# A hybrid decoder layer on one core: the attention's matmul order fixed to the source's, last products moved back, PSUM reads regrouped, and q's and k's parts written straight to their places

## The chip, the core and the metric

The kernel runs on one core of one Trainium2 chip. The metric is the device time of one execution in microseconds (us); lower is better. A core has TensorE (PE: matrix products and transposes), VectorE (DVE), ScalarE (ACT), GpSimd (POOL) and SyncE (SP: transfers). Each has its own instruction queue, and waits on the others through semaphores.

## What is computed

One layer on a sequence of 1024 positions, width 1024, everything in float32:

```python
hn = rms_norm(h, norm1_g[i])
proj = hn @ w_in[i]            # split into a_b, a_c, a_h, q, k, v, c_u, c_v
y_a = a_b * short_conv(a_c * a_h, conv_w[i])
q = rms_norm(q, per head);  k = rms_norm(k, per head)
y_b = stick_breaking_attention(q, k, v)          # 8 heads x 64
y_c = spatial_gating(gelu(c_u), gelu(c_v), ...)
h = h + concat(y_a, y_b, y_c) @ w_out[i]
h = h + square(relu(rms_norm(h, norm2_g[i]) @ w_ff1[i])) @ w_ff2[i]
h = h + sigmoid(rms_norm(h, norm3_g[i]) @ w_ple_gate[i]) * (p[i] @ w_ple_proj[i])
```

Only the attention concerns us. For a query t and the keys s < t, with z = q.k / 8, it is

```python
log_rem = where(causal, log_sigmoid(-z), 0)
suffix = cumsum of log_rem from the right, without the own term
weights = where(causal, exp(log_sigmoid(z) + suffix), 0);  o = weights @ v
```

so a weight is sigmoid(z) times the product of sigmoid(-z) over the later keys: two sigmoids, a running product from the right, and one multiplication.

## The kernel before, in words

**Number format.** A float32 operand is cut into a high and a low part (`split`, L135: ScalarE writes the high part, VectorE the difference), and a product is the three matmuls high by high, high by low and low by high (`product`, L161).

**Stages.** First come the gate's projection (`pp_ps`) and the spatial gate's (`vu_ps`, `gating`); then the stage in question, in which the attention's four pairs of heads are projected and worked on, followed by the convolution's projections; then the output projection (`o_ps`), the squared-ReLU layer (`f_ps`, `d_ps`) and the gate (`g_ps`).

**Projection, `project(pr)`, L343.** For each pair of heads the weights are loaded and split (`load_w`: `whi`, `wlo`), and for each block t of 128 positions 24 matmuls sum q, k and v of the pair into a bank `qkv_ps` (two banks, pool `ps_mm`). After that, in the source's order: ScalarE writes the squares (`qk_sq`, L373 and L374), VectorE sums them (`ss`, L377), GpSimd raises to -0.5 (`rs`, L174), VectorE scales q and k (`qk`, L382), and last v is cut into its parts (`V`, L141 by ScalarE and L142 by VectorE). `qk` and `V` read the same bank, and the tool that sets the semaphores keeps accesses of two engines to one bank in the source's order.

**Turning, `turn_qk`, L394.** After every second block q and k are transposed (`qk_tr`, L401, one of the three banks of pool `ps_tr`) and stored as operands. For head 0 an operand `QS[0]` holds q's high part in its 64 partitions and q's low part in the other 64; `KH[0]` holds k's high part twice; `KL[0]` holds k's low part and zeros; head 1 has the same with the halves exchanged. Before, whole 128-partition parts are written first (`QS[0]`, `q_lo`, `KH[0]`, and the two halves of `KL`), and after every fourth block six copies move them to their places (ScalarE L411 to L413, VectorE L414 to L416).

**Attention, `attend(pr)`, L421.** A step is a head and a group g of two query blocks t = 2g, 2g+1; the groups go 0, 1, 2, 3 for the first head and 3, 2, 1, 0 for the second. `stick` makes the weights of a step: for each t, and for each half of the keys, matmuls into a bank `z` (two banks, pool `ps_z`), two sigmoids by ScalarE (`rem`, `wt`; L454, L455), the running product by VectorE (L459), and the multiplication by VectorE or GpSimd (L462). `gather` multiplies them with v: `turn(j)` transposes four blocks of weights into a bank of `ps_tr` (`w_tr`, L484), which are split (`wT_hi`, `wT_lo`), and four to two matmuls per key block sum into `av` (L502), two turns behind; then `av` is read out. `attention` (L525) runs the stick of step i+1, then the gather of step i.

**Weaving.** Both are generators that yield after each piece with its cost in units. `weave` (L267) alternates between the attention of a pair and a filling stream: the projection of the next pair, and for the fourth pair the convolution. The projection of the first pair runs before (`alone`). `later` puts the turning 72 units behind its block; what is still waiting when a pair of heads ends is issued at once (L701). The order in which the source issues is not the order in which an engine works: a scheduler picks among what is ready by its own estimate of time, and each engine then works through its list without changing it.

## Time and profile before

| | us |
|---|---|
| median of 3 runs | 1221.15 (1217.46 to 1222.93) |
| the profiled execution | 1216.81 |
| its span, from the first to the last instruction | 1214.9 |
| busy in the span: PE / PE's weight loads (PEld) | 1191.8 / 1018.2 |
| busy in the span: DVE / ACT / POOL | 886.8 / 629.1 / 400.9 |

The attention stage lies at about 105 to 410 us. A row of the view of stretches gives the stretch, its length, then for PE, PEld, DVE, ACT and POOL the busy time in it and in brackets how many instructions started, then the clock that TensorE was granted as a share of the full one, the share of the DMA engines and GB/s. A row of the view of groups gives line, engine, operation, output and inputs with shapes, the count, the busy time and the mean duration of one in ns, and behind the second bar how long the engine stood idle before them and for what.

### The profile page before, as it was taken

How to read it: one execution, taken by the hardware profiler on the slowest of the kernel's cores; microseconds unless marked ns; L12 is line 12 of the kernel's file. 1: busy time of each engine (PE TensorE's matmuls, PEld its weight loads, DVE VectorE, ACT ScalarE, POOL GpSimd, SP SyncE). 2: the span in 40 equal slices, each digit the busy share in tenths (PEclk: the TensorE clock that was granted, in tenths of full speed). 3: DMA queues.
4: the chain of work that ended last, by engine and by line, in shares of the span. 5: the costliest groups of instructions: out<-in, count | busy, mean ns of one | idle time of the engine just before them, and what ended most of it. 6: DMA issues, size and time to landing. Idle time of an engine off the chain costs nothing.

```text
span 1214.9 us, 17743 instructions
## 1 busy us (share of the span) xinstructions
PE 1191.8 (98%) x5852; PEld 1018.2 (84%) x5852; DVE 886.8 (73%) x1310; ACT 629.1 (52%) x1244; POOL 400.9 (33%) x408
## 2 busy tenths in 40 slices
PE   9999899999999999999999999999999999999997
PEld 7899899898988888888888888888888888888886
DVE  7846888988887657877878768787665556753597
ACT  7736767667764355744333333356443444546542
POOL 3324345365343312124453544421023301013412
PEclk9999999999999999999999999999999999999998
DMA  9602359999554786779999899778889985654857
GB/s 318 222 18 94 124 166 267 247 184 171 132 116 101 164 287 207 198 194 269 251 256 251 231 261 258 217 249 277 321 248 313 279 264 171 217 163 112 179 160 208
DMA packets 127964, 254.04 MB, mean 209 GB/s; under 512 B 14496, under 2 KB 22432, under 8 KB 127168
## 3 DMA queue, kind: packets, MB, share of 16 engines
q1 hardware_dynamic: 94992, 168.08, 41.8%
q0 software_dynamic: 27664, 57.05, 25.0%
q10 hardware_dynamic: 5216, 27.79, 6.4%
q8 instruction: 46, 0.75, 0.2%
q14 instruction: 46, 0.38, 0.1%
HBM read 192.30 MB, written 92.80 MB: 235 GB/s over the span
## 4 chain that ended last, share of the span: by engine, by line
PE 86%; DVE 5%; DMA 4%; POOL 1%; issue 1%; ACT 1%; SPq 0%; ACTq 0%; DVEq 0%; POOLq 0%
PE f_ps L812 25%; PE d_ps L812 25%; PE g_ps L812 6%; PE qkv_ps L165 3%; PE qkv_ps L166 3%; PE qkv_ps L167 3%; PE av L502 2%; PE w_tr L484 2%; DVE rem L459 1%; PE vu_ps L167 1%; PE vu_ps L166 1%; PE vu_ps L165 1%; PE o_ps L167 1%; PE o_ps L165 1%; PE o_ps L166 1%
## 5 line engine op out<-in xcount | busy, mean ns | idle before, releaser
L139 DVE TENSOR_TENSOR w_lo<-raw,w_hi 128x512 fp32r<-128x512 f32 x280 | 245.1, 879 | 88.1 <-ACT w_hi L138 86.4
L138 ACT CAST w_hi<-raw 128x512 fp32r<-128x512 f32 x280 | 171.9, 619 | 232.6 <-PE d_ps L812 112.6
L812 PE MATMUL f_ps<-hn_hi,w_hi 128*128 128x512 f32 x448 | 175.1, 392 | 0.0
L812 PE MATMUL d_ps<-f_hi,w_hi 128*128 128x512 f32 x448 | 174.8, 390 | 0.0
L812 PE MATMUL f_ps<-hn_lo,w_hi 128*128 128x512 f32 x448 | 174.7, 390 | 0.0
L812 PE MATMUL f_ps<-hn_hi,w_lo 128*128 128x512 f32 x448 | 174.5, 390 | 0.0
L812 PE MATMUL d_ps<-f_hi,w_lo 128*128 128x512 f32 x448 | 174.3, 389 | 0.0
L812 PE MATMUL d_ps<-f_lo,w_hi 128*128 128x512 f32 x448 | 174.3, 389 | 0.0
L459 DVE TENSOR_TENSOR_SCAN rem<-rem 128x128 f32<-128x128 f32 (+3 forms) x64 | 90.2, 1420 | 23.0 <-ACT rem L454 22.9
L812 PEld LDWEIGHTS f_ps<-hn_lo,w_hi 128*128 128x128 f32 x448 | 84.4, 188 | 17.9 <-issue 0.2
L812 PEld LDWEIGHTS f_ps<-hn_hi,w_hi 128*128 128x128 f32 x448 | 84.5, 189 | 17.6 <-issue 0.2
L812 PEld LDWEIGHTS f_ps<-hn_hi,w_lo 128*128 128x128 f32 x448 | 84.4, 188 | 17.7
L812 PEld LDWEIGHTS d_ps<-f_hi,w_hi 128*128 128x128 f32 x448 | 84.1, 188 | 17.7 <-issue 0.2
L812 PEld LDWEIGHTS d_ps<-f_lo,w_hi 128*128 128x128 f32 x448 | 84.1, 188 | 17.6 <-issue 0.2
L812 PEld LDWEIGHTS d_ps<-f_hi,w_lo 128*128 128x128 f32 x448 | 84.1, 188 | 17.5
L165 PE MATMUL qkv_ps<-whi,xn_hi 128*128 128x384 f32 x256 | 90.4, 353 | 0.1
L167 PE MATMUL qkv_ps<-whi,xn_lo 128*128 128x384 f32 x256 | 87.8, 343 | 0.0
L166 PE MATMUL qkv_ps<-wlo,xn_hi 128*128 128x384 f32 x256 | 87.6, 342 | 0.0
L139 DVE TENSOR_TENSOR f_lo<-raw,f_hi 128x512 fp32r<-128x512 f32 x112 | 77.0, 718 | 12.6 <-ACT f_hi L138 12.2
L138 ACT CAST f_hi<-raw 128x512 fp32r<-128x512 f32 x112 | 67.0, 620 | 28.9 <-DMA raw<-f_dram 25.9
L798 POOL TENSOR_TENSOR S<-S,sq 128x512 f32<-128x512 f32 x19 | 27.4, 1440 | 157.8 <-ACT sq L874 157.8
L174 POOL TENSOR_TENSOR rs<-ss,mhalf 128x4 f32<-128x4 f32 x32 | 40.1, 1253 | 83.1 <-DVE ss L377 83.1
(252 smaller groups left out, 2704.4 us busy)
## 6 DMA issues: line engine op xcount, KB each, us to landing
raw<-in_w_ff SPq DMA_DIRECT2D x148, 256.0 KB, 4.1
raw<-f_dram SPq DMA_DIRECT2D x112, 256.0 KB, 5.1
raw<-w_sums SPq DMA_DIRECT2D x64, 256.0 KB, 3.9
f_dram<-f SPq DMA_DIRECT2D x48, 256.0 KB, 4.0
f_dram<-t SPq DMA_DIRECT2D x48, 256.0 KB, 3.7
w_sums<-in_w_ff POOLq DMA_DIRECT2D x8, 1024.0 KB, 11.6
w_sums<-w_sums POOLq DMA_DIRECT2D x8, 1024.0 KB, 13.0
raw<-in_w_out SPq DMA_DIRECT2D x28, 256.0 KB, 3.9
```

What stands on the lines that cost most here:

```text
L138: last_hi[0] = nc.scalar.copy(hi, src)
L139: low.tensor_tensor(out=lo, in0=src, in1=hi, op=ALU.subtract)
L165: nc.tensor.matmul(ps, lh, rh, start=first and i == 0, stop=False)
L166: nc.tensor.matmul(ps, lh, rl, start=False, stop=False)
L167: done = nc.tensor.matmul(ps, ll, rh, start=False, stop=last and i == len(terms) - 1)
L174: last_power[0] = nc.gpsimd.tensor_tensor(out=out, in0=in_, in1=mhalf[:, :n], op=ALU.pow)
L459: nc.vector.tensor_tensor_scan(out=back, data0=back, data1=back, initial=1.0, op0=ALU.mult, op1=ALU.bypass)
L484: nc.tensor.transpose(tr[:, n:n + P], wts[i][:, kb * P:(kb + 1) * P], ident)
L502: nc.tensor.matmul(av[:, first * P:], lhs, part[:, o:o + m], start=kb == 0 and part is hi, stop=kb == 2 * g + 1 and part is lo)
L798: return eng.tensor_tensor(out=out, in0=x, in1=y, op=ALU.add)
L812: done = nc.tensor.matmul(bank, l, r, start=first and k == 0 and i == 0, stop=k == len(b) - 1 and i == 2, skip_group_check=True)
```

## The change

1. **TensorE keeps the source's order.** Two helpers `matmul` and `transpose` remember TensorE's last instruction, and each piece that `weave` takes is issued under `tc.issue_after(last_mm[0].ins)`: its TensorE instructions stay behind all those that the source issued before. Only TensorE is held, and only inside `weave`; what is issued outside (the first pair's projection, and the turning left over at the end of a pair) may still be moved among itself, but not past the next piece of the weave.
2. **Late last products.** `gather` turns with the products two turns behind; the products of its last two turns go onto a list `rest` and are taken up one after each piece of the next stick.
3. **ScalarE first.** `V`'s high part and the squares are read from `qkv_ps` by ScalarE first, then VectorE makes `V`'s low part, the sums and `qk`.
4. **Straight to the places.** `turn_qk` writes each 64-partition part to its place: six ScalarE and four VectorE instructions a turn; `q_lo` and the six copies go.
5. **The start.** The attention's first 26 units are issued 100 units before the first pair's projection ends, and no longer counted into the first weave.

The core of the diff (the renaming of `nc.tensor.matmul` and `nc.tensor.transpose` to the helpers is left out):

```diff
+    last_mm = [None]
+    def matmul(*args, **kw):
+        last_mm[0] = nc.tensor.matmul(*args, **kw)
+        return last_mm[0]
...
     def weave(first, first_total, second, second_total):
         while True:
-            if done[0] * second_total <= done[1] * first_total:
...
+            with tc.issue_after(last_mm[0].ins):
+                if done[0] * second_total <= done[1] * first_total:
...
     def project(pr):
+            v = V[t // 2][:, t % 2]
+            ps_v = ps[:, 256:].rearrange("p (h d) -> p h d", d=HD)
+            nc.scalar.activation(v[:, :, 0], ps_v, AF.Copy, scale=r1[t])
             sq = half_tmp("qk_sq", (P, 4, HD + 1))
...
+            nc.vector.scalar_tensor_tensor(out=v[:, :, 1], in0=ps_v, scalar=r1[t], in1=v[:, :, 0],
+                                           op0=ALU.mult, op1=ALU.subtract)
             ss = small.tile([P, 4], F32, tag="ss", name=name("ss"))
...
-            split(ps[:, 256:].rearrange("p (h d) -> p h d", d=HD), v[:, :, 0], v[:, :, 1], scale=r1[t])
...
     def turn_qk(head, t, qk):
-        split(tr[:, :256], QS[0][th][:, ws], low_q[th][:, ws], scale=gq)
-        nc.scalar.activation(KH[0][th][:, ws], tr[:, 256:], AF.Copy, scale=gk)
-        for hh, own in enumerate((lo_p, hi_p)):
-            nc.vector.scalar_tensor_tensor(out=KL[hh][th][own, ws], in0=tr[own, 256:],
...
-        if t % 4 == 3:
-            nc.scalar.copy(KH[1][th][hi_p], KH[0][th][hi_p])
...
-            nc.vector.tensor_copy(QS[0][th][hi_p], low_q[th][lo_p])
+        for hh, own, other, q, k in heads_of:
+            nc.scalar.activation(QS[hh][th][own, ws], q, AF.Copy, scale=gq[own])
+            for part in (own, other):
+                nc.scalar.activation(KH[hh][th][part, ws], k, AF.Copy, scale=gk[own])
+        for hh, own, other, q, k in heads_of:
+            nc.vector.scalar_tensor_tensor(out=QS[hh][th][other, ws], in0=q, scalar=gq[own],
+                                           in1=QS[hh][th][own, ws], op0=ALU.mult, op1=ALU.subtract)
+            nc.vector.scalar_tensor_tensor(out=KL[hh][th][own, ws], in0=k, scalar=gk[own],
+                                           in1=KH[hh][th][own, ws], op0=ALU.mult, op1=ALU.subtract)
...
     def gather(hh, g):
-            for j in range(-2, g + 1):
...
+            for j in range(g + 1):
+                *parts, n = turn(j)
+                turned.append(parts)
+                yield 2 * n + 10
+                if j > 1:
+                    multiply()
+                    yield 8
+            rest.extend([multiply] * len(turned))
...
     def attention():
+        def weights(nxt, *step):
+            for units in parts[nxt][0](*step):
+                yield units
+                if rest:
+                    rest.pop(0)()
+                    yield 8
...
+    for _ in take(alone, GATING + PROJECT - 100):
+        pass
+    attending = attention()
+    for _ in take(attending, AHEAD):
+        pass
     for _ in alone:
         pass
```

Both programs do the same 5800 TensorE instructions. In TensorE's list the first 379 and the last 3531 are the same; all that moves lies between, from the first pair's projection to the convolution.

**Place 1: TensorE, first pair of heads, where the first head's group 3 meets the second head's.** Before (L447 to L453 are `z`, L484 the turned weights, `wt_361` and `wt_369` the weights of blocks 6 and 7):

```order
L447 MATMUL z_386_1704<-KH_232_957,QS_267_1159 128x512
L449 MATMUL z_386_1704<-KL_227_951,QS_267_1159 128x512
L447 MATMUL z_395_1732<-KH_268_1160,QS_267_1159 128x512
L449 MATMUL z_395_1732<-KL_263_1154,QS_267_1159 128x512
L453 MATMUL z_395_1732<-below_104,ident_99 128x128
L447 MATMUL z_396_1738<-KH_232_957,QS_267_1159 128x512
L449 MATMUL z_396_1738<-KL_227_951,QS_267_1159 128x512
L484 MATMUL w_tr_397_1751<-ident_99,wt_369_1614 128x128
```

And now (L136 is the helper `matmul`, so all products have its line):

```order
L136 MATMUL z_385_1717<-KL_262_1158,QS_265_1162 128x512
L136 MATMUL z_385_1717<-below_104,ident_99 128x128
L136 MATMUL z_386_1723<-KH_231_956,QS_265_1162 128x512
L136 MATMUL z_386_1723<-KL_227_951,QS_265_1162 128x512
L136 MATMUL qkv_ps_392_1742<-whi_300_1385,xn_hi_36_200 128x384
L136 MATMUL qkv_ps_392_1742<-wlo_301_1386,xn_hi_36_200 128x384
L136 MATMUL qkv_ps_392_1742<-whi_300_1385,xn_lo_37_201 128x384
```

Before, three scores `z` and the next turned weights stand one behind the other, without a projection product between them; now six projection products follow each pair of scores (three are shown), and the turned weights stand two such groups later.

**Place 2: TensorE, where the first pair's projection ends.** Before (`qk_tr_291` is the turning of blocks 6 and 7, `qkv_ps_326` the first block of the second pair's projection, 24 rows long; a row of dots leaves rows out):

```order
L453 MATMUL z_335_1449<-below_104,ident_99 128x128
L401 MATMUL qk_tr_291_1331<-ident_99,qk_285_1291 128x128 x2
L484 MATMUL w_tr_336_1465<-ident_99,wt_293_1348 128x128
L484 MATMUL w_tr_336_1465<-ident_99,wt_328_1422 128x128 x2
L165 MATMUL qkv_ps_326_1414<-whi_296_1359,xn_hi_36_200 128x384
...
L401 MATMUL qk_tr_291_1331<-ident_99,qk_285_1291 128x128 x2
```

And now (`qkv_ps_291` is block 7 of the first pair, `qkv_ps_329` the second pair's first block):

```order
L136 MATMUL qkv_ps_291_1323<-whi_224_945,xn_lo_143_524 128x384
L140 MATMUL qk_tr_295_1358<-ident_99,qk_290_1321 128x128 x4
L136 MATMUL z_298_1375<-KH_229_954,QS_228_953 128x384
L136 MATMUL z_298_1375<-KL_226_949,QS_228_953 128x384
L136 MATMUL z_298_1375<-below_104,ident_99 128x128
L136 MATMUL qkv_ps_329_1439<-whi_300_1385,xn_hi_36_200 128x384
```

Before, the second half of the turning (that of block 7) stood behind the 24 products of the next projection; now all of it follows block 7's last product at once, and everything else of the weave stands behind it.

**Place 3: VectorE, a turning in the first pair's round.** Before (`q_lo`, `KL` and the copies belong to `qk_tr_431`; `rem_424` is a running product, `wt_425` a multiplication):

```order
L142 SCALAR_TENSOR_TENSOR q_lo_323_1411<-qk_tr_431_1902,c_gq_119,QS_322_1410 128x256
L459 SCALAR_TENSOR_TENSOR rem_424_1870<-rem_424_1870 128x768
L462 TENSOR_TENSOR wt_425_1871<-wt_425_1871,rem_424_1870 128x767
L407 SCALAR_TENSOR_TENSOR KL_319_1405<-qk_tr_431_1902,c_gk_121,KH_321_1409 64x256
L407 SCALAR_TENSOR_TENSOR KL_320_1407<-qk_tr_431_1902,c_gk_121,KH_321_1409 64x256
L414 COPY QS_324_1412<-QS_322_1410 64x512
L415 COPY QS_324_1412<-q_lo_323_1411 64x512
```

And now:

```order
L424 SCALAR_TENSOR_TENSOR QS_325_1435<-qk_tr_430_1919,c_gq_119,QS_325_1435 64x256
L426 SCALAR_TENSOR_TENSOR KL_323_1431<-qk_tr_430_1919,c_gk_121,KH_326_1436 64x256
L424 SCALAR_TENSOR_TENSOR QS_327_1437<-qk_tr_430_1919,c_gq_119,QS_327_1437 64x256
L426 SCALAR_TENSOR_TENSOR KL_324_1433<-qk_tr_430_1919,c_gk_121,KH_328_1438 64x256
L149 TENSOR_TENSOR wT_lo_439_1959<-w_tr_437_1953,wT_hi_438_1958 128x512
```

Before, a running product and its multiplication stood between the two reads of the turning's bank; now its four reads follow one another.

More of the change, by code (lines that the diff above doesn't have):

```diff
@@ L164, in product @@
         for i, ((lh, ll), (rh, rl)) in enumerate(terms):
-            nc.tensor.matmul(ps, lh, rh, start=first and i == 0, stop=False)
-            nc.tensor.matmul(ps, lh, rl, start=False, stop=False)
-            done = nc.tensor.matmul(ps, ll, rh, start=False, stop=last and i == len(terms) - 1)
+            matmul(ps, lh, rh, start=first and i == 0, stop=False)
+            matmul(ps, lh, rl, start=False, stop=False)
+            done = matmul(ps, ll, rh, start=False, stop=last and i == len(terms) - 1)
         return done
@@ L518, in gather @@
-            low = half_tmp("av_lo")
-            nc.scalar.copy(low[:HD], av[HD:])
-            nc.vector.tensor_tensor(out=yb[g // 2][own, (g % 2) * 256:(g % 2 + 1) * 256],
-                                    in0=av[:HD], in1=low[:HD], op=ALU.add)
+                        matmul(av[:, first * P:], lhs, part[:, o:o + m],
+                               start=kb == 0 and part is hi,
+                               stop=kb == 2 * g + 1 and part is lo)
+                if kb == 2 * g + 1:
+                    evict()
@@ L542, in attention @@
             if i % 2 == 1:
+                parts[pr][2]()
+            if i == len(steps) - 1:
+                while rest:
+                    rest.pop(0)()
+                    yield 8
                 parts[pr][2]()
@@ L702, in hybrid_block @@
             emitted[0] += waiting.pop(0)[1]()
[L703 removed]
+        weave(attending, ATTEND - (AHEAD if pr == 3 else 0), fill,
               PROJECT if pr < 3 else CONVOLVE * 0.72)
```

113 lines of the change are left out of this document (53 added, 60 removed).

## Prediction

> **What bounds the kernel now.** I read the stretches first (columns: the stretch, its length, busy time and count of PE, PEld, DVE, ACT and POOL, TensorE's clock, DMA). In the attention stage, ten us each:
>
> ```profile
> core 0: us, PE busy (x) PEld busy (x) DVE busy (x) ACT busy (x) POOL busy (x), PEclk, DMA share, GB/s
> 120.00:130.00 10.00, 8.81 (x59) 8.46 (x57) 8.84 (x18) 7.13 (x19) 4.26 (x5) 1.00 0.58 197
> 140.00:150.00 10.00, 7.42 (x45) 5.43 (x43) 9.55 (x12) 9.27 (x24) 4.26 (x5) 1.00 0.01 2
> 150.00:160.00 10.00, 9.71 (x54) 9.62 (x55) 8.23 (x11) 3.46 (x9) 2.44 (x3) 0.83 0.00 0
> 200.00:210.00 10.00, 10.00 (x62) 9.61 (x62) 6.46 (x8) 5.83 (x14) 2.60 (x3) 1.00 0.88 299
> 210.00:220.00 10.00, 7.31 (x44) 5.76 (x43) 9.46 (x13) 8.84 (x24) 7.93 (x8) 0.93 0.80 138
> 220.00:230.00 10.00, 10.00 (x62) 9.82 (x61) 8.19 (x11) 3.85 (x10) 3.01 (x3) 0.90 1.00 184
> 260.00:270.00 10.00, 9.21 (x61) 8.89 (x60) 8.86 (x17) 6.07 (x16) 4.43 (x5) 1.00 1.12 230
> 270.00:280.00 10.00, 10.00 (x65) 9.38 (x63) 6.70 (x8) 6.48 (x17) 4.03 (x4) 1.00 0.88 166
> 280.00:290.00 10.00, 7.21 (x44) 5.58 (x43) 9.28 (x12) 8.94 (x22) 7.93 (x8) 1.00 0.85 142
> 340.00:350.00 10.00, 10.00 (x55) 8.37 (x55) 7.81 (x10) 5.54 (x13) 3.90 (x5) 1.00 0.55 136
> 360.00:370.00 10.00, 8.81 (x47) 6.80 (x46) 10.00 (x12) 3.46 (x9) 8.09 (x5) 1.00 0.77 155
> ```
>
> TensorE is the bound where nothing goes wrong: in 200 to 210 and 220 to 230 it is busy throughout. Once in each round of a pair of heads (at 140, 210 and 280, so a round is 70 us) it starts only 43 to 45 products in 10 us instead of 62, while DVE and ACT are at their fullest; just before that, in 200 to 210 and 270 to 280, DVE has 3 us to spare. The work of both is there in the sum; it lies badly. Whom TensorE waits for there, in the waits by engine (us in total, times, longest), and how the second place looks in the timeline (start, length, in brackets the idle time before and its releaser):
>
> ```profile
> PE w_tr L484 <- DVE KL L407: 4.6, 3, 1.7
> PE w_tr L484 <- DVE wt L462: 2.8, 4, 1.2
> PE z L447 <- ACT wt L455: 2.4, 7, 0.7
> PE z L447 <- DVE QS L416: 0.8, 1, 0.8
> 216.68 0.27 PE L453 MATMUL z<-below,ident 128*128 128x128 f32 x1
> 218.66 1.11 PE L484 MATMUL w_tr<-ident,wt 128*128 128x128 f32 x4 [1.71 <-DVE KL L407]
> 219.43 0.67 PE L165 MATMUL qkv_ps<-whi,xn_hi 128*128 128x384 f32 x1
> 221.82 0.42 PE L166 MATMUL qkv_ps<-wlo,xn_hi 128*128 128x384 f32 x1
> 300.38 0.33 PE L167 MATMUL qkv_ps<-whi,xn_lo 128*128 128x384 f32 x1
> 300.55 0.34 PE L165 MATMUL qkv_ps<-whi,xn_hi 128*128 128x384 f32 x1
> ```
>
> The largest wait is for a bank of `ps_tr` that a turning still holds: its last reads, `KL`, stand in DVE's list behind a running product and its multiplication (place 3). The scheduler had put scores and turned weights in a row without projection products between them (place 1), so TensorE has nothing else to do. And behind the wait the clock falls: from 219.43 to 221.82 seven products start, 0.34 us apart, where 0.17 us is the pace at 300.38.
>
> **What the change gives back.** How much a bad stretch loses I read from the weight loads, one per product: 9.8 us of them in a full stretch of a round (9.82 at 220), 8.4 with the convolution (8.37 at 340). At 140, 210 and 280 it is 4.4, 4.0 and 4.2; at 120, 260 and 360 it is 1.3, 0.9 and 1.6. That is 16.4 us. [...] PE's own busy column would give 11.2 us for the same six rows, and a sum 5.2 us higher; the counts (44 products instead of 62 at 210) agree with the loads.
>
> The slow clock adds seven times 0.17 us at 220; 150 to 160 shows the like (0.83), 290 does not: 2 x 1.2 = 2.4 us. [...]
>
> Why should these go? In the new order six projection products stand between any two pieces of the attention, about 1 us of work each time, so scores and turned weights no longer queue up; the turning's bank is read without a running product in between; the late last products leave `wT_lo` one more stick of time; and the wait on the copy L416 has lost its copy. What is late next is DVE. Two rounds, and rows of the groups between 105 and 410 us:
>
> ```profile
> 140.00:210.00 70.00, 67.14 (x433) 64.07 (x432) 60.00 (x91) 49.41 (x125) 32.77 (x33) 0.98 0.63 188
> 210.00:280.00 70.00, 66.52 (x431) 63.45 (x429) 60.01 (x91) 47.98 (x126) 37.13 (x37) 0.98 0.90 201
> L407 DVE SCALAR_TENSOR_TENSOR KL<-qk_tr,c_gk,KH 64x256 fp32r<-64x256 f32 x28 | 13.4, 480 | 2.2 <-ACT KH L405 1.7
> L142 DVE SCALAR_TENSOR_TENSOR q_lo<-qk_tr,c_gq,QS 128x256 fp32r<-128x256 f32 x14 | 6.6, 473 | 1.3 <-ACT QS L141 1.3
> L414 DVE CAST QS<-QS 64x512 fp32r<-64x512 f32 x7 | 3.3, 468 | 0.0
> L405 ACT ACTIVATE KH<-qk_tr,c_gk 128x256 fp32r<-128x256 f32 x14 | 6.7, 479 | 2.2 <-DVE q_lo L142 1.7 <-issue 0.2
> L411 ACT CAST KH<-KH 64x512 fp32r<-64x512 f32 x7 | 4.3, 617 | 0.2
> ```
>
> DVE has 60.0 us of work in a round. A round has four turnings; DVE drops four `q_lo` (1.9 us) and six copies (at most 2.8 us) and gains eight differences at 0.48 (3.8 us), so 59 us. Shortened by the 4 to 6 us a round above, a round of 65 us has DVE at 91%. ACT drops 4 x 2 x 0.48 + 6 x 0.62 = 7.6 us and gains 24 x 0.48 = 11.5 us: 53 of 65 us. Both still fit, so I take the 18.8 us as given back in full, and down to 70% of it (13.2 us) as the lower bound, since DVE at 91% in a fixed order must now and then be late.
>
> **What the change adds.** First, place 2: the turning of blocks 6 and 7 follows block 7's last product at once, and the fixed order holds the whole weave behind it. Until `qk` of block 7 is there TensorE has nothing. The chain, by its rows in the same stretch:
>
> ```profile
> L141 ACT ACTIVATE V<-qkv_ps,r 128x128 fp32r<-128x128 f32 x27 | 9.9, 372 | 16.5 <-DVE qk L382 16.4
> L374 ACT ACTIVATE qk_sq<-qkv_ps 128x256 f32<-128x256 f32 x27 | 10.6, 393 | 9.1 <-PE qkv_ps L167 8.4
> L142 DVE SCALAR_TENSOR_TENSOR V<-qkv_ps,r,V 128x128 fp32r<-128x128 f32 x27 | 9.1, 347 | 3.0 <-ACT V L141 2.6
> L377 DVE TENSOR_REDUCE ss<-qk_sq 128x4 f32<-128x260 f32 x27 | 11.1, 412 | 2.8 <-ACT qk_sq L374 2.7
> L174 POOL TENSOR_TENSOR rs<-ss,mhalf 128x4 f32<-128x4 f32 x27 | 35.1, 1298 | 66.9 <-DVE ss L377 66.9
> L382 DVE TENSOR_TENSOR qk<-qkv_ps,rs 128x256 f32<-128x256 f32 x27 | 11.2, 416 | 7.5 <-POOL rs L174 7.3
> L139 DVE TENSOR_TENSOR wlo<-stage,whi 128x384 fp32r<-128x384 f32 x23 | 17.6, 770 | 0.7 <-ACT whi L138 0.6
> ```
>
> 0.37 + 0.39 + 0.35 + 0.41 + 1.30 + 0.42 = 3.2 us. If `V`'s low part runs beside the squares, 2.9; if two weight splits (2 x 0.77) and block 6's `qk` stand in DVE's list where GpSimd's 1.3 us run, 3.9. I take 3.5, nearer the upper end, since those splits do stand there. A slow clock behind it: 0 to 1.2 us by 219.43 to 221.82; this wait is longer than any there, so 1.2. [...]
>
> Second, the end of the first pair: `qk_tr_526` stands only seven attention rows and six projection products behind block 7's last product, about 1.7 us at the pace of 300.38 (0.17 us for 384 columns). The same chain of 3.2 to 3.9 us leaves 1.5 to 2.2; I take 1.8. At the ends of the second and third pair the later half of the turning stands 4.1 and 3.6 us behind, counted likewise: nothing. What queues behind a waiting transpose is all of TensorE, so DVE and ACT catch up meanwhile.
>
> Third, the scores have two banks. At some ten places the second score of a block comes about 2 us after the one whose bank it needs, and four sigmoids must be through first:
>
> ```profile
> L455 ACT ACTIVATE wt<-z 128x512 f32<-128x512 f32 x48 | 29.6, 617 | 0.0
> ```
>
> 4 x 0.62 = 2.5 us, less about the half us by which the first two of them start earlier, is just hidden; each other ACT instruction in between costs up to 0.6 us. So 0 to 6 us; I take 0.2 each, 2.0, as ACT is only three quarters full.
>
> The order of `V` and the squares, on ACT: 16.4 us of ACT's waiting for `qk` go, off TensorE's path; worth nothing by itself. The earlier start takes two scores from the weave's beginning; its gain is in the row at 120. All behind the convolution is in the same order, so nothing is costed there. The larger transfers of the stage go with the attention's steps and come earlier with it.
>
> **Sum.** Profiled execution 1216.8 - 16.4 - 2.4 + 3.5 + 1.2 + 1.8 + 2.0 = 1206.5, a gain of 10.3. The median of the runs is 4.3 above the profiled execution; 1221.15 - 10.3 gives 1211. With the worst of all bounds, -13.2 + 3.9 + 1.2 + 2.2 + 6.0 is +0.1, no gain; the forecast's own range is 1207 to 1221.
>
> **Rivals.**
>
> A, slower: DVE is held at the turnings. In its list the first of the four reads needs ACT's part, and since both read one bank it may wait for all six ACT instructions, 6 x 0.48 = 2.9 us, where before it waited for one. Behind it stand the running products and so the turned weights. In a round DVE has 65 - 59 = 6 us to spare, 1.5 us for each of four turnings; all 16 turnings above that cost TensorE's time. At 2.9 us: 16 x 1.4 = 22 us, 1233. The change is lost from 1.5 + 10.3/16 = 2.1 us a turning on. For it: DVE at 91%. Against it: DVE runs behind ACT when it is full, and the waits in the `KL` and `q_lo` rows (2.2 and 1.3 us over 42 instructions) are small. Chance 0.12.
>
> B, no change: DVE's 9.3 to 9.6 us in the bad stretches are real work, and half of the 18.8 us returns as waits elsewhere; with the added 8.5 the gain is 0.9: 1220. For it: DVE at 10.00 in 360 to 370, where the new order cannot help. Against it: the 3 us that DVE has free just before each place. Chance 0.27.
>
> C, all of it: the scores' waits and the slow clock at the start do not come, the other two at their lower bounds: 18.8 - 2.9 - 1.5 = 14.4, 1207 or below. Chance 0.14.
>
> That the change doesn't do what it says is settled by the order: the six products do stand between. The forecast keeps 0.47.
>
> **The numbers.** Half a per cent (6.1 us, below 1215.0 or above 1227.3) is about what a measurement of this kernel can tell from no change. Faster: three quarters of the forecast (0.35), C (0.14) and some of B (0.06), 0.55. Slower: A beyond its point and a little of B, 0.15. Same: 0.30. The range for 8 in 10 runs from below C's 1207 to the middle of A: 1203 to 1225.
>
> **What would show it.** Right: in the changed profile no stretch between 130 and 300 us under 9 us of weight loads, PEclk 1.00 there, no wait of `w_tr` for `KL`, rounds of about 65 us; one new idle time of 3 to 4 us on TensorE near 115 us before `qk_tr`, and a smaller one near 180. Wrong: DVE waiting for ACT at its `QS` rows by over 2 us each (A); DVE over 9.5 in most stretches with TensorE's idle time spread over many short waits (B); no wait before the first pair's last `qk_tr`.

## The result, and the profile after

The changed kernel takes 1255.15 us (median of 4 runs, 1252.45 to 1256.19), the kernel before 1219.31 us on the same chip: a ratio of 1.0289 (95% interval 1.0253 to 1.0325), 35 us slower. The prediction said 1211 and held a loss for the least likely case. The span of the profiled execution grows from 1214.9 to 1250.7 us, by 35.8.

The attention stage of the changed kernel in stretches (columns as in the prediction):

```profile
110.00:120.00 10.00, 6.03 (x32) 5.23 (x32) 6.63 (x15) 7.43 (x20) 6.26 (x8) 0.87 0.24 69
120.00:130.00 10.00, 8.77 (x42) 8.18 (x41) 7.26 (x10) 6.95 (x16) 2.74 (x2) 0.79 0.85 301
...
190.00:200.00 10.00, 6.53 (x34) 6.01 (x33) 5.38 (x10) 6.30 (x18) 4.99 (x7) 0.83 1.11 244
...
220.00:230.00 10.00, 7.65 (x44) 6.42 (x43) 7.17 (x12) 7.09 (x18) 2.83 (x3) 1.00 1.12 205
230.00:240.00 10.00, 6.88 (x40) 6.55 (x39) 8.50 (x10) 3.27 (x8) 6.28 (x6) 0.84 0.66 120
...
260.00:270.00 10.00, 10.00 (x74) 9.89 (x74) 6.16 (x10) 7.34 (x20) 2.01 (x4) 1.00 0.60 212
270.00:280.00 10.00, 7.65 (x39) 7.30 (x37) 9.97 (x15) 6.36 (x19) 9.53 (x13) 0.72 0.68 126
...
350.00:360.00 10.00, 6.06 (x22) 4.44 (x21) 7.13 (x15) 4.10 (x12) 2.76 (x4) 0.66 0.62 168
```

Before, one stretch in each round was bad; now, of those shown, only 260 to 270 has the 9.8 us of weight loads of a full one. The bad ones are no longer mainly those in which DVE is full. In 190 to 200 DVE works 5.4 of 10 us, in 220 to 230 7.2. Of the rows shown, only 270 to 280 has both a full DVE and a slow TensorE. The rows shown are mostly bad ones: the clock is below 1.00 in six of these eight, but in only two of the other 22 up to 410 us.

The whole stage, first before, then after:

```profile
105.00:410.00 305.00, 292.67 (x1792) 268.75 (x1791) 246.92 (x369) 195.09 (x481) 141.90 (x133) 0.99 0.69 166
```

```profile
105.00:410.00 305.00, 266.58 (x1588) 244.52 (x1588) 236.37 (x334) 193.70 (x486) 133.93 (x121) 0.96 0.64 153
```

TensorE starts 204 instructions fewer in the same 305 us, and DVE does less, not more. Whom TensorE waits for in the changed kernel (us in total, times, longest), and the wait for `wT_lo` before:

```profile
PE av L136 <- DVE wT_lo L149: 17.1, 15, 3.1
PE qk_tr L140 <- DVE qk L399: 8.2, 5, 3.5
PE R_ps L136 <- DVE diag L212: 3.9, 1, 3.9
PE w_tr L140 <- DVE KL L426: 3.3, 1, 3.3
PE w_tr L140 <- DVE wT_lo L149: 2.8, 2, 2.4
...
PE z L136 <- ACT wt L466: 1.3, 4, 0.5
```

```profile
PE av L502 <- DVE wT_lo L139: 1.6, 3, 0.9
```

These six and one of 1.3 us for `qkv_ps` are 37.9 us; before, the four rows in the prediction and this one are 12.2. The 25.7 us between them, and the clock, (0.99 - 0.96) x 305 = 9 us, make 35, as much as the whole loss. (The part of the clock is rough: some of the slow time lies inside the waits.) The largest row, 17.1 of the 37.9 us where before it was 1.6, is one that the prediction never priced: the products with v waiting for the low part of the turned weights.

How such waits come about, by the timeline of DVE (and one row of ACT) at two places of the changed kernel. First the end of the first pair, where TensorE waits from 192.7 to 196.2 us for `qk`; then 234.2 to 237.3, where it waits for `wT_lo`:

```profile
192.66 0.70 DVE L149 TENSOR_TENSOR wlo<-stage,whi 128x384 fp32r<-128x384 f32 x1
193.29 0.54 DVE L149 TENSOR_TENSOR wT_lo<-w_tr,wT_hi 128x384 fp32r<-128x384 f32 x1
194.46 0.51 ACT L148 CAST whi<-stage 128x384 fp32r<-128x384 f32 x1 [1.43 <-DMA stage<-in_w_qkv]
195.00 0.76 DVE L149 TENSOR_TENSOR wlo<-stage,whi 128x384 fp32r<-128x384 f32 x1 [1.17 <-ACT whi L148]
195.68 0.41 DVE L399 TENSOR_TENSOR qk<-qkv_ps,rs 128x256 f32<-128x256 f32 x1
...
231.46 0.42 DVE L399 TENSOR_TENSOR qk<-qkv_ps,rs 128x256 f32<-128x256 f32 x1 [0.86 <-POOL rs L184]
231.80 3.53 DVE L470 TENSOR_TENSOR_SCAN rem<-rem 128x1024 f32<-128x1024 f32 x1
235.43 1.23 DVE L473 TENSOR_TENSOR wt<-wt,rem 128x1023 f32<-128x1023 f32 x1
236.57 0.68 DVE L149 TENSOR_TENSOR wT_lo<-w_tr,wT_hi 128x512 fp32r<-128x512 f32 x1
```

The piece that TensorE waits for stands behind a weight split, or behind a running product and its multiplication. The split waits for ScalarE, and ScalarE waited 1.43 us for weights that were still on their way: GpSimd's `rs` was done at 194.4, so 1.3 us of this wait are the transfer and the split ahead of `qk`. The running product took 3.53 us here, where four of the eight of its size take 2.3. DVE idles 1.17 us in the first and 0.86 us in the second place: it isn't short of time, the wanted piece is just not next in its list.

### The profile page after: what moved, and what is told of

It reads as the page before. It is cut to its first block, busy times and chain, and to the rows that moved or that the text cites. A ratio compares the mean times of both kernels' runs of the same rounds, so it can differ in the third digit from the quotient of the medians.

```text
span 1250.7 us, 17789 instructions
## 1 busy us (share of the span) xinstructions
PE 1200.2 (96%) x5852; PEld 1023.2 (82%) x5852; DVE 892.8 (71%) x1302; ACT 642.3 (51%) x1284; POOL 405.6 (32%) x408
## 4 chain that ended last, share of the span: by engine, by line
PE 71%; DVE 6%; DMA 5%; issue 3%; ACT 2%; POOL 2%; ACTq 0%; DVEq 0%; SPq 0%; POOLq 0%
PE d_ps L854 24%; PE f_ps L854 22%; PE g_ps L854 6%; PE cv_ps L136 5%; PE qkv_ps L136 3%; PE o_ps L136 3%; PE av L136 2%; PE z L136 2%; PE w_tr L140 1%; DVE rem L470 1%; DMA y_both<-y_both 1%; DMA raw<-in_w_out 1%; POOL rs L184 1%; DVE wT_lo L149 1%; DMA raw<-in_w_ff 1%
## 5 line engine op out<-in xcount | busy, mean ns | idle before, releaser
L470 DVE TENSOR_TENSOR_SCAN rem<-rem 128x128 f32<-128x128 f32 (+3 forms) x64 | 97.5, 1530 | 26.1 <-ACT rem L465 25.7
L136 PE MATMUL qkv_ps<-whi,xn_hi 128*128 128x384 f32 x256 | 93.6, 366 | 1.3 <-DVE qk L399 1.3
L136 PE MATMUL qkv_ps<-wlo,xn_hi 128*128 128x384 f32 x256 | 88.2, 344 | 0.0
L136 PE MATMUL qkv_ps<-whi,xn_lo 128*128 128x384 f32 x256 | 88.1, 344 | 0.0
L473 POOL TENSOR_TENSOR wt<-wt,rem 128x127 f32<-128x127 f32 (+4 forms) x40 | 45.6, 1158 | 94.0 <-DVE rem L470 61.4
```

The source lines that it names most:

```text
L136: last_mm[0] = nc.tensor.matmul(*args, **kw)
L470: nc.vector.tensor_tensor_scan(out=back, data0=back, data1=back, initial=1.0, op0=ALU.mult, op1=ALU.bypass)
L473: done = (nc.vector if on_vector else nc.gpsimd).tensor_tensor(out=wt[:, :W - 1], in0=wt[:, :W - 1], in1=rem[:, 1:W], op=ALU.mult)
```

## The experiments

The theories at the start. **O**: the held order itself costs, since TensorE can no longer pull other products forward while a result is late. **T**: the turnings cost, DVE waiting for all six ScalarE instructions (the prediction's rival A). **B**: it takes both. The kernels ran in five sets, each beside the kernel before, so ratios are compared, not medians; a difference of ratios is given in us by 1218 us for the kernel before.

| kernel | parts, order | median us | ratio to before (95%) |
|---|---|---|---|
| changed | 1 to 5 | 1255.15 | 1.0289 (1.0253 to 1.0325) |
| only_order | 1 | 1266.59 | 1.0394 (1.0366 to 1.0422) |
| only_direct | 4 | 1211.39 | 0.9945 (0.9924 to 0.9965) |
| no_order | 2 to 5 | 1226.53 | 1.0071 (1.0050 to 1.0093) |
| no_direct | 1, 2, 3, 5 | 1246.08 | 1.0230 (1.0195 to 1.0264) |
| hold_attention | all, attention held | 1254.13 | 1.0293 (1.0261 to 1.0324) |
| hold_fill | all, filling held | 1218.14 | 1.0012 (0.9996 to 1.0028) |
| late_turn | all, last turning later | 1248.49 | 1.0243 (1.0217 to 1.0269) |
| carry | all, longer way to v | 1250.02 | 1.0267 (1.0241 to 1.0293) |
| held_short_scan | all, half the running product | 1237.73 | 1.0168 (1.0143 to 1.0193) |
| held_eased2 | all, three places mended | 1241.53 | 1.0197 (1.0172 to 1.0222) |
| held_eased | the same without 4 | 1258.33 | 1.0326 (1.0309 to 1.0343) |
| no_sfirst | 1, 2, 4, 5 | 1252.72 | 1.0293 (1.0268 to 1.0317) |
| direct_sfirst | 3, 4 | 1227.57 | 1.0074 (1.0049 to 1.0099) |
| direct_vmid | 4, half of 3 | 1215.12 | 0.9987 (0.9971 to 1.0002) |
| direct_late | 2, 4 | 1215.11 | 0.9975 (0.9961 to 0.9990) |
| direct_turn | 4, last turning later | 1231.05 | 1.0098 (1.0081 to 1.0115) |
| direct_fill | 4, filling held | 1218.64 | 1.0003 (0.9989 to 1.0017) |
| only_direct_again | 4 | 1211.02 | 0.9944 (0.9929 to 0.9959) |

### Which part costs: order or turnings

One part alone on the kernel before, and one part taken from the changed kernel. **only_order** is before with `tc.issue_after` in `weave` and nothing else:

```diff
+            with tc.issue_after(last_mm[0].ins):
                 if done[0] * second_total <= done[1] * first_total:
```

> The kernel before with part 1 alone: TensorE's order held to the source's inside the weave, nothing else. Theory T (the turnings cost: VectorE waits for six ScalarE instructions at each of them, 31.9 us in the changed profile): there are no such turnings here, so within 10 us of before, 1209 to 1229. Theory O (the held order costs: TensorE can no longer pull projection products forward while VectorE is late): most of the 36 us is here already, 1240 to 1260. Theory B (it takes both together): 1215 to 1230.

**only_direct** is before with the new body of `turn_qk`; **no_order** is the changed kernel with the line above taken out again; **no_direct** is the changed kernel with the old `turn_qk` and its copies.

> The kernel before with part 4 alone: q's and k's parts written straight to their places, the scheduler free. Theory T: VectorE waits for ScalarE at the turnings by some 20 to 32 us, of which it has some 30 us to spare over the stage, so 1230 to 1250. Theory O: the scheduler moves other products into the waits, 1212 to 1226. Theory B: 1215 to 1230.

> The changed kernel without part 1: the scheduler orders TensorE as before, all other parts stay. Theory T: the waits at the turnings stay, 1240 to 1257. Theory O: back to before or below, 1205 to 1225. Theory B: 1215 to 1230.

> The changed kernel without part 4: the turnings with whole parts and six copies as before, the order held, all other parts stay. Theory T: the 31.9 us of VectorE's waits go, 1205 to 1225. Theory O: still slow, 1240 to 1260. Theory B: 1215 to 1230.

Part 1 alone costs 3.9%, 48 us, more than the whole change and more than O's band; without it the loss shrinks from 2.9 to 0.7%. Part 4 alone gains 0.55%. So O holds in the main, and T is not the main cause. O's bands are not met throughout: no_order's 1226.5 lies just above O's and inside B's, so something else costs in the free order too (the last of these sections). Parts 2, 3 and 5 together are worth 20 us to the held order (only_order against no_direct). The first waits of only_order between 100 and 410 us, then of only_direct:

```profile
PE av L136 <- DVE wT_lo L149: 25.3, 24, 2.1
PE qk_tr L140 <- DVE qk L393: 5.4, 3, 3.8
```

```profile
PE qkv_ps L165 <- DVE V L142: 4.3, 5, 1.8
PE av L498 <- DVE wT_lo L139: 1.4, 3, 0.8
```

T's mechanism is there all the same. What DVE idles before the turning's first reads, by the groups of the changed kernel and of only_direct:

```profile
L424 DVE SCALAR_TENSOR_TENSOR QS<-qk_tr,c_gq,QS 64x256 fp32r<-64x256 f32 x30 | 14.5, 483 | 29.4 <-ACT KH L422 29.1
```

```profile
L409 DVE SCALAR_TENSOR_TENSOR QS<-qk_tr,c_gq,QS 64x256 fp32r<-64x256 f32 x30 | 14.5, 483 | 13.0 <-ACT KH L407 12.6
```

Thirty `QS` instructions are fifteen turnings: 2.0 us of idle time a turning with the held order, 0.9 with the free one. In a free order the part gains although DVE waits. In the held one such a turning also delays what TensorE waits for next. At the start of the stage DVE idles from 110.2 to 113.4 us for the six ScalarE instructions, and the sums of block 6 stand behind its four reads:

```profile
113.38 0.48 DVE L424 SCALAR_TENSOR_TENSOR QS<-qk_tr,c_gq,QS 64x256 fp32r<-64x256 f32 x1 [3.20 <-ACT KH L422]
```

TensorE then waits 3.51 us, to 118.4, for block 6's `qk`. Over the whole kernel with the order held, the one with part 4 is 0.6% above the one without, with intervals that touch: a cost of some 7 us there is likely but not firm.

### Which held list costs: the attention's or the filling's

**hold_attention** remembers the last TensorE instruction of the attention alone and puts only the attention's pieces behind it; **hold_fill** does so for the filling stream.

```diff
-            with tc.issue_after(last_mm[0].ins):
...
+                with tc.issue_after(mine.ins):
+                    got = next(first, None)
...
+                done[1] += next(second, 1000)
```

> All five parts, but only the attention's pieces are kept in the source's order among themselves; the projection's and the convolution's products may be placed anywhere by the scheduler. Theory O (the held order costs because filling products can't be moved to where VectorE is late): about the level of the kernel without part 1, 1226 us (1219 to 1234), and TensorE's wait of the products with v for wT_lo falls from 17 us to below 7. Rival H (keeping the attention's own order is what costs: turned weights and products with v can't change places when a result is late): 1243 or more, with the wait for wT_lo above 12 us.

> All five parts, but only the filling products (projection, convolution and the turnings) are kept in the source's order among themselves; the attention's pieces may be placed anywhere. The counterpart to holding the attention alone, which cost as much as holding all. If it is the attention's places that cost: near the kernel without part 1, 1221 to 1233, TensorE's waits for wT_lo below 7 us. If any held list costs: 1240 or more.

Theory O in its first form falls: with the projection's products free to go anywhere, the attention held among itself costs as much as everything held (1.0293 against 1.0289). With the filling held and the attention free, nothing is lost against before (1.0012), less than either expectation said. So holding the attention's own pieces is what costs. (How much of that is TensorE's list itself stays open: the scheduler also sets the other engines' lists anew for each version, and between no_order and the changed kernel only about two thirds of DVE's instructions of the stage keep their order. No run holds the one and frees the other.) The waits of hold_attention, and of hold_fill:

```profile
PE av L136 <- DVE wT_lo L149: 13.3, 11, 1.9
PE av L136 <- ACT wT_hi L148: 8.6, 5, 3.3
```

```profile
PE av L136 <- DVE wT_lo L149: 6.9, 8, 2.1
PE qk_tr L140 <- DVE qk L402: 4.9, 3, 4.0
```

Are the parts later in the held kernels, or asked for earlier? For each of the 80 turns I set two times side by side: the work that stands in TensorE's list between the last transpose of the turn and its first product with v (0.17 us for 384 columns and 0.11 for a transpose, medians between two starts in the stage of before and of the changed kernel; other widths in proportion, an estimate; no waits), and the time from the start of `wT_hi` to the end of `wT_lo` in the profiled execution.

| kernel | work between, mean us | parts take, mean us | turns in which the parts take longer |
|---|---|---|---|
| before | 4.55 | 2.30 | 5 |
| only_direct | 5.25 | 2.63 | 7 |
| hold_fill | 4.93 | 2.69 | 9 |
| changed | 4.28 | 2.67 | 18 |
| hold_attention | 4.84 | 2.81 | 16 |
| only_order | 2.90 | 2.91 | 45 |

The parts take 2.3 to 2.9 us everywhere. What sorts these six kernels is the last column (call these turns short): 5 to 9 in the three without a loss, 16 to 45 in the three with one. Before, TensorE also had more work ahead of a product where the parts came late (correlation of the two columns over the turns 0.43, and -0.24 in the changed kernel), but this does not sort the others: by the same reckoning it is 0.14 in hold_fill and in hold_attention alike, and 0.30 in only_order. How the free order comes by fewer short turns is not shown.

### Can the held order be mended

**late_turn** takes out the place at which the last turning of a pair is issued at once:

```diff
-        while waiting:
-            emitted[0] += waiting.pop(0)[1]()
...
+                later(54 if t == 7 else 72, lambda t=t, qk=qk: turn_qk(heads[pr], t, qk))
```

> All five parts, but the last turning of each pair's projection is no longer issued at once at the pair's end: it is put 54 units behind its block, in among the next pieces. Theory P (single places cost: the waits for qk of 3.9 us near 115 and 3.7 us near 192, and a halved clock of about 2 us behind each): both waits go and the time falls by 8 to 12 us, to 1243 to 1247. Rival L (VectorE is late all along, so that what is not waited for there is waited for at the next piece): it falls by less than 4 us, 1251 or more.

The ratio falls by 0.0046, 5.6 us, half of what theory P asked, between the two bands, and the intervals overlap a little. The stall near 115 us is not gone: `qkv_ps`, whose bank is held until `qk` has read it, waits 4.1 us, to 121.3, in its place.

**carry** lets the last two products of a step wait for two turns of the next step:

```diff
+                rest.append(multiply)
                 yield 2 * n + 10
-                if j > 1:
-                    multiply()
+                if len(rest) > 2:
+                    rest.pop(0)()
                     yield 8
```

> All five parts and the held order, but the products with v of a step's last two turns are no longer taken up in the next stick: they wait until the next gather has turned two more. Between a turn and its product then stand, by the durations of TensorE's own work in its list, at least 4.0 us (median 7.1) where there stood at least 1.8 (median 4.3). From the last transpose of a turn to the end of its wT_lo it takes 3.2 us on the mean and 5.2 at the ninth tenth in the changed kernel. Theory D (the distance is what the held order costs: the parts are no later than in the free order, but the place is fixed): the wait for wT_lo falls from 17 us to below 5, and the time by 10 to 18 us, to 1237 to 1245. Rival L (VectorE is late whatever it is asked for): the waits move to KL, qk and wT_lo before the turned weights, and the time stays at 1249 or above.

```profile
PE qkv_ps L136 <- DVE qk L399: 7.6, 3, 3.5
PE av L136 <- ACT y_both L521: 4.8, 5, 2.4
...
PE qk_tr L140 <- DVE qk L399: 4.1, 2, 3.5
...
PE av L136 <- DVE y_b L530: 3.5, 2, 2.1
...
PE av L136 <- DVE wT_lo L149: 1.8, 3, 0.7
```

Both theories are half right. The wait for `wT_lo` falls from 17.1 to 1.8 us, as D said; the time falls by 2.7 us by the ratio, less than the measurement can tell, as L said. The waits moved: to the bank of `av`, which `y_both` and `y_b` now read out late (8.3 us), and to `qk` (11.7 us in its two rows, 9.5 in the changed kernel). By the reckoning above, carry has at most 6 short turns left of 80. So few short turns are not enough: the largest row of waits can go, and the loss stays.

**held_short_scan** makes the running product over the later half of the keys only, so that DVE has less to do:

```diff
-                back = rem[:, :W][:, ::-1]
+                back = rem[:, W // 2:W][:, ::-1]
```

> All five parts and the held order, but the running product leaves out the earlier half of the keys of each block (its instructions are half as long), so that VectorE has some 35 to 45 us less to do in the stage; TensorE's work and order are the same. If TensorE's loss in the held order is waiting for VectorE's results, it falls with VectorE's queue: the waits for wT_lo to below 8 us, the time to 1225 to 1240. If the loss lies in the order itself (chains of ScalarE and GpSimd, the ends of the pairs, the slow clock): within 10 us of 1255.

```profile
PE qk_tr L140 <- DVE qk L399: 9.9, 5, 4.4
PE av L136 <- DVE wT_lo L149: 5.4, 6, 1.4
...
PE R_ps L136 <- DVE diag L212: 3.8, 1, 3.8
```

As expected of waiting for VectorE: 15 us of the 35 go with DVE's shorter list, and two thirds of the wait for `wT_lo`. But 20 us stay, though DVE now has 209 us of work in 305, and the waits for `qk` and `diag` do not shrink. They do not go by DVE's load. The longest of them, 4.4 us, ends at 195.6 where ScalarE had waited 2.6 us for a transfer of weights and DVE for ScalarE; the chains behind the others I did not follow.

**held_eased** and **held_eased2** put carry, late_turn and a free weave with the convolution together:

```diff
-            with tc.issue_after(last_mm[0].ins):
+            with tc.issue_after(last_mm[0].ins) if hold else ExitStack():
...
+              hold=pr < 3)
```

> The held order with its single places mended together: products with v carried over (alone worth 5 us), the last turning of a pair put 54 units behind its block (7 us), part 4 left out (9 us), and the weave with the convolution left free (the wait of the second R_ps for diag, 4 us and a slow clock behind it). Theory S (the held order costs as a sum of places, each of which can be mended): the savings add up, 1223 to 1234. Rival L (what is not waited for at one place is waited for at the next): half of them or less, 1240 or above. In neither case below the free order's 1211.

Without part 4 nothing is won: the scores of a pair now stand close behind the late turning, and the copies that complete their operands are slow to come. (The scores of the first head's blocks 4 and 5 are even issued ahead of these copies there, so they are of incomplete operands.) Its two largest waits:

```profile
PE qkv_ps L136 <- DVE qk L402: 16.5, 9, 6.1
PE z L136 <- DVE QS L431: 13.4, 3, 5.0
```

> All five parts and the held order, with products carried over (alone worth 5 us), the last turning 54 units behind its block (7 us) and the weave with the convolution left free (a wait of 4 us and the slow clock behind it, some 6 us). Theory S (a sum of places): 1234 to 1241. Rival L (the waits come back at other places): 1244 or above.

With part 4 the loss falls from 2.89 to 1.97%, by 11 us where the three mends alone were priced at 18. Just outside S's band and nearer to it than to L's: the loss is in part a sum of places, in part it moves on. 24 us of it I did not mend; its largest waits are `qkv_ps` for `qk` (11.8 us) and `av` for `y_both` (9.7 us). Of the latter, 8.3 us are one wait, to 217.75. ScalarE itself stood idle ahead of it, and the profile names the landing of a transfer as what released it:

```profile
216.18 0.59 ACT L148 CAST wT_hi<-w_tr 128x512 fp32r<-128x512 f32 x1 [7.68 <-DMA y_dram<-y_both]
```

The profiled execution took 1244.8 us, and two of the four took 1238, so this wait may not come each time. Where the rest lies stays open.

### What the other parts do when the order is free

> The kernel before with part 4 (straight to the places) and part 2 (late last products), order left to the scheduler. The kernel without part 1 is 15 us above the one with part 4 alone, so parts 2, 3 and 5 cost 15 us together in a free order. If part 2 is what costs (the scheduler takes the late products for less urgent and moves the next turned weights ahead of them): 1220 to 1227. If it is part 3 or 5: 1208 to 1214, and if late products help by themselves, below 1208.

> The kernel before with part 4 (straight to the places) and part 3 (ScalarE first at the projection's bank), order left to the scheduler. If part 3 is what costs in the free order (V's low part stands ahead of the sums, and so of qk, in VectorE's list, and the two banks of the projection come free later): 1218 to 1227. If it is part 2 or 5: 1207 to 1214.

Part 2 on top of part 4 costs 0.3%, 3.7 us, with intervals that just touch, and lands between the bands. Part 3 costs 1.3%, 16 us, as much as parts 2, 3 and 5 lose together (15 us). Part 3's edit here is the one in the change (`V`'s high part ahead of the squares, its low part ahead of the sums). The costs do not simply add, and part 5 was not run alone. **direct_vmid** makes half of part 3:

```diff
                                  AF.Square, scale=HD ** -0.5)
+            nc.scalar.activation(v[:, :, 0], ps_v, AF.Copy, scale=r1[t])
...
                 in1=rs.unsqueeze(2).broadcast_to([P, 4, HD]), op=ALU.mult)
+            nc.vector.scalar_tensor_tensor(out=v[:, :, 1], in0=ps_v, scalar=r1[t], in1=v[:, :, 0],
+                                           op0=ALU.mult, op1=ALU.subtract)
```

> The kernel before with part 4, order left to the scheduler, and half of part 3: ScalarE writes V's high part directly behind the squares (no longer waiting for qk), VectorE writes V's low part last, behind qk, as before. If part 3 costs because VectorE makes V's low part ahead of the sums and qk: no loss here, 1206 to 1213. If it costs because of ScalarE's copy or the scheduler's estimates: 1218 or above, like the kernel with all of part 3.

Between the two bands, 5 us above part 4 alone. So most of part 3's cost comes with its other half, `V`'s parts ahead of the squares and sums. In direct_sfirst, DVE before a wait of 4.0 us for `qk`:

```profile
119.18 0.35 DVE L390 SCALAR_TENSOR_TENSOR V<-qkv_ps,r,V 128x128 fp32r<-128x128 f32 x1
119.45 0.41 DVE L393 TENSOR_REDUCE ss<-qk_sq 128x4 f32<-128x260 f32 x1
...
120.37 0.55 DVE L149 TENSOR_TENSOR wlo<-stage,whi 128x384 fp32r<-128x384 f32 x1
120.83 1.48 DVE L469 TENSOR_TENSOR_SCAN rem<-rem 128x640 f32<-128x640 f32 x1
122.23 0.40 DVE L398 TENSOR_TENSOR qk<-qkv_ps,rs 128x256 f32<-128x256 f32 x1
```

That one wait is quoted from one execution; that the later `qk` makes all 16 us is argued, not shown. In the held order part 3 changes nothing:

> All parts but the third: V's parts are written after qk again, as before. With the scheduler free this part cost 16 us. If it costs by the order of VectorE's reads (V's low part ahead of the sums, so qk later), it does so in the held order as well, where the waits for qk near 115, 192, 273 and 281 us stand open: 1235 to 1245. If it cost in the free order only by what the scheduler made of it, the time is within 5 us of the changed kernel's 1255.

1.0293 without it, 1.0289 with it. The waits for `qk` grow from 8.2 to 12.1 us and those for `wT_lo` fall from 17.1 to 12.0.

**direct_turn** (part 4 and late_turn's edit), **direct_fill** (part 4 and hold_fill's edit) and the repeat look for a better kernel:

> The kernel before with part 4 alone, order free, and the last turning of a pair's projection put 54 units behind its block instead of at the pair's end. Part 4 alone gave 1211 (0.9945 of before), with its largest waits on TensorE (2.1 us near 133, 2.4 us near 189) at the ends of the first and second projection. If those come from the turning's place: 1207 to 1210. If the scheduler moves the turning to the same place anyway: 1210 to 1213.

> The kernel before with part 4, and only the filling products (projection, convolution, turnings) kept in the source's order among themselves. With all five parts, holding the filling alone was 8 us faster than holding nothing. If that carries over: 1203 to 1208. If it was worth 8 us only because part 3's late qk was put at a worse place by the scheduler: 1209 to 1214.

> The kernel before with part 4 alone once more, to firm up the version that is faster than both: 1211 (0.9945 of before, 0.9924 to 0.9965); a ratio above 0.998 would say that its gain isn't firm.

Neither expectation was met for direct_turn or for direct_fill. The first loses 1.5% against part 4 alone, and its TensorE waits 3.1 us, to 263, for `qk` and 3.2 us for weights that DVE hasn't multiplied. Holding the filling was worth 7 us with all five parts and costs 7 us on part 4 alone. So single edits in a free order move the time by several us either way through what the scheduler makes of them. Part 4 alone is firm at 0.9944 (0.9929 to 0.9959): it beats both kernels, by 7 and by 42 us.

## Why the prediction was wrong

**What bounds the kernel.** Right, and it stays right: TensorE in the good stretches, its waits for DVE in the bad ones. The weight loads went with the count of products more closely than PE's busy time in the two stretches compared here: 9.89 us for 74 in 260 to 270 of the changed kernel and 6.42 for 44 in 220 to 230, where PE is busy for 10.00 and 7.65.

**"So I take the 18.8 us as given back in full."** This step failed. It rested on "DVE at 91%" of a shorter round and on "both still fit": sums of work. None of that decides in a fixed list. What decides whether TensorE waits is, for each result, whether TensorE's own work ahead of its use is longer than the chain behind it, and I asked this only of the turnings of q and k. The products with v, the most frequent such use, have no term in the sum; the table of 80 turns has 18 of them short where before had 5. Means wouldn't have shown it (4.55 us of work between before, 4.28 after): it has to be asked turn by turn, against DVE's list in the changed kernel. Measured: 25.7 us more of waits and 9 us more lost to the clock, where 18.8 were to be gained. That holding TensorE's order costs is shown (only_order, no_order, hold_attention, hold_fill). That the short turns are how it costs is shown only in part: carry removes nearly all of them and wins 2.7 us, since the next late results then end TensorE's waits.

**"The late last products leave `wT_lo` one more stick of time."** True of these two turns of each step: only_order has 45 short turns, the changed kernel 18, and parts 2, 3 and 5 together are worth 20 us there. Part 3 is worth nothing there (no_sfirst), so it is part 2 or 5; no run separates the two. It isn't enough.

**The places that were priced.** The start: 3.5 us predicted, 3.5 and 0.3 measured. The size is right partly by luck: the first wait is for block 6's `qk`, late because DVE was held at the turning before (3.20 us, rival A's mechanism), which the sum left out. The slow clock behind it: 1.2 predicted, (1 - 0.79) x 10 = 2.1 measured in 120 to 130. The end of the first pair: 1.8 predicted, 3.5 measured, since two weight splits and `wT_lo` stood between `ss` and `qk`, the second split waiting for its weights; I had put splits into the first place and left them out of the second. The ends of the later pairs: nothing predicted, 1.3 and 0.7 us measured near 275 and 282. The scores' banks: 2.0 predicted, 1.3 measured. Together some 4 us off, a tenth of the error of 44.

**"No wait of `w_tr` for `KL`".** Wrong: one of 3.3 us is left, twice as long as the longest before.

**The convolution**, for which nothing was costed: 3.9 us for `diag` at its beginning, and a clock of 0.66 in 350 to 360. Its products are the same, in the same order, but what stands ahead of `diag` on DVE is not.

**"The order of `V` and the squares ... worth nothing by itself."** Wrong in a free order, where it costs up to 16 us; right in the held one.

**The rivals.** A named the right side and a real wait: its row shows 2.0 us a turning, near the 2.1 at which it was to decide. But DVE wasn't full, the turnings explain some 7 us (no_direct, not firm), and A would not have given 1255. B's form, many waits spread over the stage, came true, without its sign that DVE is over 9.5: and more waits came than were removed. No rival said that the fixed list alone loses 48 us.

## What to carry to other kernels

Before an in-order list is fixed by hand, set for every result that crosses engines the work ahead of its use against the whole chain behind it, queues of the other engines included, and count the uses that fall short; busy shares do not tell. Do so for every kind of result, not only the one with the largest wait: here mending that one alone won 2.7 of 35 us. Follow each chain to its start, which at the end of the first pair was a transfer of weights. A scheduler's list that looks bunched may still be the better one, so hold one stream at a time and measure each. Test the parts of a bundle alone: here one part gains 0.55% and the bundle loses 2.9%.

## What the runs showed of the hardware

In the changed kernel the length of a single wait does not say whether TensorE's clock falls. Behind a wait of 3.33 us TensorE runs at full pace (the clock is 1.00 in 250 to 260), and behind two of 1.04 and 1.31 us, 0.9 us apart, at half of it (0.50 in each of the six microseconds from 275 to 281):

```profile
252.50 0.63 PE L140 MATMUL w_tr<-ident,wt 128*128 128x128 f32 x4 [3.33 <-DVE KL L426]
...
253.15 0.34 PE L136 MATMUL qkv_ps<-wlo,xn_hi 128*128 128x384 f32 x1
253.32 0.34 PE L136 MATMUL qkv_ps<-whi,xn_lo 128*128 128x384 f32 x1
```

```profile
272.87 0.39 PE L136 MATMUL av<-wT_lo,V 128*128 128x256 f32 x1 [1.04 <-DVE wT_lo L149]
...
275.11 0.69 PE L136 MATMUL qkv_ps<-whi,xn_hi 128*128 128x384 f32 x1 [1.31 <-DVE qk L399]
275.60 0.52 PE L136 MATMUL qkv_ps<-wlo,xn_hi 128*128 128x384 f32 x1
275.92 0.52 PE L136 MATMUL qkv_ps<-whi,xn_lo 128*128 128x384 f32 x1
```

At 253 products start 0.17 us apart, at 275 0.32, and so on until 280.6, the last one before the next wait.

In its stage, up to 410 us, the view of stretches has the clock at 0.50 in 117.43 to 124.26, 195.94 to 199.35, 236.90 to 240.31, 274.44 to 281.27 and 352.95 to 359.78 us, 27.3 us in all, and at 1.00 between these. Of TensorE's five waits of over 3 us there, four have such a fall inside them (3.51 us to 118.37, 3.46 to 196.15, 3.12 to 237.31 and 3.94 to 354.56), and the wait of 3.33 us has none. The fall at 274.44 lies inside the wait of 1.31 us, while no fall lies at single waits of 2.44 us, to 306.14, and of 2.21, to 320.36. What decides it is not shown.

A 64-partition read of 256 columns takes DVE 0.48 us (the `QS` row above), as long as the 128-partition one of before (473 ns): here halving the partitions saved nothing, and two halves took 0.97 us where one whole took 0.47.
